# Dense work at the ends of attention heads, and decode scores in two PSUM banks

## The chip, the cores and the metric

The kernel runs on one core of a Trainium2 chip. The metric is the device time of one execution in microseconds (us); before the change it is 1550.55 us, the median of three runs (1549.25 to 1555.3).

## The reference

One inference step of a one-layer encoder with two kinds of input: a prompt of 1024 frames, and 8 decode streams with 16 new frames each and a cache of 512 past frames. The layer has two parallel head groups, 4 heads of differential softmax attention and 4 heads of retention; they come from one input projection and feed one output projection. A gated MLP with a convolution of width 3 follows, and a final RMSNorm. The part that the change touches is the attention:

```python
def diff_attention_block(q, k, v, q_pos, k_pos, rel_bias, lam):
    bias = ...                                                  # T5 buckets, per head
    visible = (k_pos[None, :] // CHUNK) <= (q_pos[:, None] // CHUNK)
    def probs(qi, ki):
        s = jnp.einsum('bqhd,bkhd->bhqk', qi, ki) * A_QK_DIM ** -0.5 + bias
        return jax.nn.softmax(jnp.where(visible, s, NEG_INF), axis=-1)
    p = probs(q[..., :64], k[..., :64]) - lam * probs(q[..., 64:], k[..., 64:])
    return jnp.einsum('bhqk,bkhd->bqhd', p, v)
# prompt: 8 query blocks of 128 for each head, over keys 0 .. end of the block
# decode: for each of 8 streams, 16 queries over 512 cached and 16 new keys
```

## The kernel before

TensorE (PE) takes its instructions in the order in which the code writes them from the start of the attention stage on (`manual_schedule` for PE). The order on the other engines and on the DMA queues is made by a planner that simulates the program; it can bring a load or a copy forward as far as buffers allow. SP issues most loads, ACT's queue the stores of evacuated rows.

Between the steps of attention and decode the code calls `fill(ns)`. It puts dense work, the input projections, on PE: units in a list, cut into steps of three matmuls. A step of a `k` or `q` unit (24 steps, 384 columns) is entered as 480 ns, one of a `kr`, `qr` or `gr` unit (72 steps, 256 columns) as 320 ns. `prog["lim"]` says how many units may have been started: where the limit is reached, `fill` puts nothing on PE. `drain(n)` does all steps until n units are done. `later(ns, fn)` writes `fn` when the entered time has moved on by ns. All dense work that attention and decode do not use is done in the retention stage that follows, where `fill` is called too, until it runs out.

Attention (lines 684 to 712) runs over 32 blocks, n_ = 8 * head + block. In each round it writes `scores` of the next block, a fill, `flip` of this block (transposes of the probabilities, L649), a fill, `weighted` (the product with V, L661), a fill. `scores` (L626) needs two PSUM buffers `sc`, one for each half of the differential softmax; DVE adds the bias (L629) and takes the maximum (L631), ACT the exponential (L632), DVE merges the halves (L637), and only then can `flip` run. After blocks 3 and 7 the four outputs are normalised and `heads_out` is due (`later`): 4 transposes (L670), a scaled copy on ACT (L672), and a store to d_m. Before the first block of the next head, `drain(2 * h2 + 2)` finishes that head's k and q units, and `load_v` loads its V into `vt`, of which there is one buffer. The two units that follow the k and q units, `kr` and `qr`, are done in the last head.

Then the pool of attention is closed and that of decode opened in its place. The last `qr` unit's weights are half in the new pool (`with_extra(dp)`); the cached keys of stream 0 (`kc`, 1 MB) go there too. `fill(9000)` covers their load. Decode runs over 8 streams. For each, `dflip` writes 4 transposes of the cached keys for each head (L744), copies them to SBUF (ACT for odd heads, L746, DVE for even, L748) and fills 400 after each head; then `dflip2` of the stream before (products of the probabilities `e` with `dm`, L773, and of its 16 new keys, L776), `dscore` (L756), a fill, `dout` of the stream before (L790), a fill. The PSUM buffers `tp` that L744, L773, L776 and L790 write are two.

In retention (line 988 on) the decode rows come first: for each of 8 streams a `fill(2000)`, 8 products with its state (L1018), 8 products for the new state (L1023), the update on DVE (L1026), the store, and the load of the state three streams on (L1044). There are three state buffers.

Of the kernel before, what the change touches and what calls it, by code (L numbers as in the profile page):

```python
# [7 lines left out]
F32 = mybir.dt.float32  # L8
# [3 lines left out]
ALU = mybir.AluOpType  # L12
# [36 lines left out]
def body(ctx: ExitStack, tc: tile.TileContext, i):  # L49
# [485 lines left out]
    with ExitStack() as st:  # L535
# [73 lines left out]
            units.append([lambda: load_wt(base, h * 128), lambda w_: dense_t(nm, h, w_), None])  # L609

        def load_v(h):
            vt = ap.tile([128, 8, 128], F32, tag="vt", bufs=1, name="vt")
            nc.sync.dma_start(vt, i["v_prompt"][:, h * 128:h * 128 + 128].rearrange("(t p) d -> p t d", p=128))
            return vt

# [39 lines left out]
        def weighted(h, vt, qb, e, sm, pTs):  # L655
            if qb % 4 == 0:
                o4s[0] = ap.tile([128, 4, 128], F32, tag="o4", bufs=2, name="o4")
            o4 = o4s[0]
            po = tp()[:, 0]
            for n in range(qb + 1):  # L660
                T.matmul(po[:, 0:128], lhsT=pTs[n // 4][:, n % 4], rhs=vt[:, n], start=(n == 0), stop=(n == qb))  # L661
            V.tensor_scalar_mul(o4[:, qb % 4], po[:, 0:128], sm[:, 4:5])
            if qb % 4 == 3:
                small_norm(ap, o4, 4)
                later(5000, lambda: heads_out(h, qb, o4))

        def heads_out(h, qb, o4):
            p_ = tp()
# [10 lines left out]
        def spare():  # L679
# [5 lines left out]
        drain(2)  # L685
        vt = load_v(0)
        cur = (0, vt, 0) + scores(0, kqs[0], 0)
        f_scores = ([1500, 1250, 1150, 1200, 650, 850, 450, 650],
                    [1950, 1850, 1750, 1650, 1550, 1450, 1350, 1250])
        f_flip = ([1925, 1775, 1625, 1475, 1325, 1325, 1475, 1025],  # L690
# [3 lines left out]
        for n_ in range(8 * NH):  # L694
            h, qb = divmod(n_, 8)
            nxt = None
            if n_ < 8 * NH - 1:
                h2, qb2 = divmod(n_ + 1, 8)
                if qb2 == 0:
                    drain(2 * h2 + 2)  # L700
                    vt = load_v(h2)
                nxt = (h2, vt, qb2) + scores(h2, kqs[h2], qb2)
            prog["lim"] = 10 if n_ >= 23 else n_ // 8 * 2 + 4
            fill(f_scores[h // 3][qb])
            pTs = flip(*cur)
            fill(f_flip[h // 3][qb])
            weighted(*cur, pTs)
            fill(f_out[h // 3][qb])
            cur = nxt
# [4 lines left out]
    with ExitStack() as st:  # L714
# [19 lines left out]
            nc.sync.dma_start(vn, i["v_sample"][b * TD:(b + 1) * TD])  # L734
            vcs[b] = vc, vn

        def dflip(b):
            KT = dp.tile([128, NH, PAST + TD], F32, tag="KT", bufs=2, name="KT")
            kc = kcs.pop(b)
            G.tensor_copy(KT[:, :, PAST:], knT[:, :, b * TD:(b + 1) * TD])  # L740
            for h in range(NH):
                p_ = tp()
                for n in range(4):
                    T.transpose(p_[:, n], kc[:, n, h * 128:h * 128 + 128], ident)  # L744
                if h % 2:
                    S.copy(KT[:, h, 0:PAST], p_.rearrange("p a b -> p (a b)"))  # L746
                else:
                    V.tensor_copy(KT[:, h, 0:PAST], p_.rearrange("p a b -> p (a b)"))  # L748
                fill(400)
            return KT  # L750

        def dscore(b, KT):
            s_ = pva.tile([128, 1024], F32, tag="sc", bufs=2, name="sc")
            for (c0, c1) in ((0, 512), (512, 528)):
                for h in range(NH):
                    T.matmul(s_[32 * h:32 * h + 32, c0:c1], lhsT=qbd[:, h, b].rearrange("p a t -> p (a t)"),  # L756
                             rhs=KT[:, h, c0:c1], start=True, stop=True, skip_group_check=True)
            sm = dp.tile([128, 4], F32, tag="sm", bufs=3, name="sm")
            nk = PAST + TD
            V.tensor_tensor(out=s_[:, 384:nk], in0=s_[:, 384:nk], in1=nbs, op=ALU.add)  # L760
            V.tensor_reduce(out=sm[:, 0:1], in_=s_[:, 0:nk], op=ALU.max, axis=AX.X, negate=True)
            e = dp.tile([128, nk], F32, tag="e", bufs=2, name="e")
            S.activation(out=e, in_=s_[:, 0:nk], func=ACTF.Exp, bias=sm[:, 0:1], scale=1.0, accum_out=sm[:, 1:2])
            V.reciprocal(out=sm[:, 2:3], in_=sm[:, 1:2])
            dm = dp.tile([128, 128], F32, tag="dm", bufs=1, name="dm")
            V.tensor_scalar(out=dm, in0=seld, scalar1=sm[:, 2:3], scalar2=lamcol, op0=ALU.mult, op1=ALU.mult)
            return e, dm
# [40 lines left out]
        load_k(0)  # L808
        prog["rope"] = dp.tile([128, NT, 2, 64], F32, name="rope")
        nc.sync.dma_start(prog["rope"], i["rope"].rearrange("(t p) a d -> p t a d", p=128))  # L810
        fill(9000)
        nbs = dp.tile([128, 144], F32, name="nbs")
        p_ = tp().rearrange("p a b -> p (a b)")
        T.matmul(p_[:, 0:144], lhsT=anti16[0:64], rhs=hk, start=True, stop=True)
# [2 lines left out]
        for b in range(NB + 1):  # L817
            if b < NB:
                if b + 1 < NB:
                    load_k(b + 1)  # L820
                load_vc(b)
                KT = dflip(b)
            if last:
                pT = dflip2(*last)
            fill(0)
            nxt = (b,) + dscore(b, KT) if b < NB else None
            fill(1200 if b else 1500)
            if last:
                dout(last[0], pT)
            fill(1000)  # L830
            last = nxt
        while pend:
            fill(500)
# [818 lines left out]
```

## Time and profile before

| | |
|---|---|
| median of three runs | 1550.55 us |
| the profiled execution | 1549.34 us |
| its span | 1547.6 us |
| PE busy | 1509.1 us, 98% of the span |
| DVE, ACT, POOL busy | 963.7 us, 600.7 us, 232.3 us |
| chain that ended last, by engine | PE 86%, DVE 5%, DMA 4% |

The span is the time from the first to the last instruction in the profile. PE is busy nearly everywhere, so the change can only move the time by the idle time of PE that it closes or opens, and by what PE itself has more or less to do. Attention reaches from about 184 to 457 us, decode from there to about 557 us, retention to about 650 us.

### The profile page before, as it was taken

What the parts mean: (1) busy time and instruction counts of PE and PEld (TensorE: products, weight loads), DVE (VectorE), ACT (ScalarE), POOL (GpSimd) and SP (SyncE); (2) the same over time, 40 slices, a digit from 0 to 9 for tenths busy, and PEclk for the clock granted to TensorE, in tenths of its full rate; (3) what the DMA queues carried; (4) which work ended last, traced back from release to release, by engine and by line L of the source; (5) the groups of instructions that cost most, each with busy time, mean ns of one, the idle gap of its engine ahead of it and who ended that gap; (6) DMA issues with size and microseconds to landing.
All of it is one profiled execution on the core that took longest, in us unless ns stands there. A gap on an engine that the chain in (4) does not pass through costs nothing.

```text
span 1547.6 us, 27019 instructions
## 1 busy us (share of the span) xinstructions
PE 1509.1 (98%) x10580; PEld 1375.5 (89%) x10580; DVE 963.7 (62%) x1735; ACT 600.7 (39%) x1167; POOL 232.3 (15%) x335
## 2 busy tenths in 40 slices
PE   6999999999999999999999999999999999999998
PEld 5867899999998999888899999999999988888786
DVE  5701247888864533653489777877787758254695
ACT  4501125555322432555565443444444345021212
POOL 2000021111221111433202101110111100000051
PEclk9999999999999999999999999999999999999999
DMA  9965331111329655685532222222222238132232
GB/s 296 276 253 182 114 104 49 55 51 53 107 83 328 226 201 176 221 259 194 176 117 87 70 79 77 75 71 79 72 79 71 79 112 276 36 116 87 95 134 109
DMA packets 191515, 205.98 MB, mean 133 GB/s; under 512 B 11357, under 2 KB 149899, under 8 KB 191388
## 3 DMA queue, kind: packets, MB, share of 16 engines
q1 hardware_dynamic: 172412, 189.31, 37.5%
q10 hardware_dynamic: 18976, 14.95, 3.0%
q8 instruction: 83, 1.36, 0.3%
q14 instruction: 44, 0.36, 0.1%
HBM read 154.66 MB, written 49.56 MB: 132 GB/s over the span
## 4 chain that ended last, share of the span: by engine, by line
PE 86%; DVE 5%; DMA 4%; ACT 1%; SPq 1%; issue 1%; POOL 0%; ACTq 0%; POOLq 0%; DVEq 0%
PE dn L62 10%; PE dn L64 10%; PE dn L63 10%; PE pb L1339 5%; PE pb L1341 5%; PE pb L1340 5%; PE pf L64 3%; PE pf L62 3%; PE pf L63 3%; PE dn L1339 2%; PE dn L1341 2%; PE dn L1340 2%; PE tp L1339 2%; PE tp L1341 2%; PE tp L1340 2%; PE tp L63 2%
## 5 line engine op out<-in xcount | busy, mean ns | idle before, releaser
L62 PE MATMUL dn<-w,hhi 128*128 128x256 f32 x648 | 190.1, 293 | 0.0
L64 PE MATMUL dn<-w,hlo 128*128 128x256 f32 x648 | 181.6, 280 | 0.0
L63 PE MATMUL dn<-w,hhi 128*128 128x256 f32 x648 | 181.4, 280 | 0.0
L62 PEld LDWEIGHTS dn<-w,hhi 128*128 128x128 f32 x648 | 122.4, 189 | 12.0 <-issue 10.2
L64 PEld LDWEIGHTS dn<-w,hlo 128*128 128x128 f32 x648 | 122.4, 189 | 7.5 <-issue 7.5
L63 PEld LDWEIGHTS dn<-w,hhi 128*128 128x128 f32 x648 | 122.5, 189 | 4.3 <-issue 4.2
L1285 DVE SCALAR_TENSOR_TENSOR y<-U,cv,y 128x1168 f32<-128x1168 f32 x88 | 124.3, 1429 | 3.0 <-ACT y L1282 2.1
L58 ACT CAST sl<-raw 128x512 fp32r<-128x512 f32 x65 | 40.3, 622 | 108.2 <-PE pb L1340 93.5
L58 ACT CAST se<-raw 128x512 fp32r<-128x512 f32 x66 | 41.0, 624 | 100.5 <-PE dn L1340 48.4
L62 PE MATMUL dn<-hhi,w 128*128 128x384 f32 x192 | 69.4, 361 | 0.0
L246 POOL TENSOR_TENSOR sg<-sg,rot 128x256 f32<-128x256 f32 x36 | 28.1, 781 | 272.1 <-DVE rot L245 230.4
L64 PE MATMUL dn<-hhi,w 128*128 128x384 f32 x192 | 64.6, 336 | 0.0
L63 PE MATMUL dn<-hlo,w 128*128 128x384 f32 x192 | 64.5, 336 | 0.0
L1291 POOL COPY tails<-U 128x18 f32<-128x18 f32 x44 | 23.1, 526 | 270.8 <-DVE U L1356 182.1
L1282 ACT ACTIVATE y<-U,cv 128x1168 f32<-128x1168 f32 x44 | 60.2, 1367 | 4.5 <-DVE U L1360 0.5
L1511 DVE TENSOR_TENSOR facc<-facc,pf 128x512 f32<-128x512 f32 x54 | 36.8, 681 | 39.1 <-PE pf L64 39.0
L59 DVE TENSOR_TENSOR w<-raw,w 128x512 fp32r<-128x512 f32 x56 | 38.9, 709 | 35.7 <-ACT w L58 23.6
L632 ACT ACTIVATE e<-sc,sm 128x128 f32<-128x128 f32 (+7 forms) x64 | 47.4, 744 | 30.9 <-DVE sm L631 30.1
L62 PE MATMUL dn<-woh,mh 128*128 128x512 f32 x144 | 57.9, 402 | 0.0
L58 ACT CAST ew<-wr 128x512 fp32r<-128x512 f32 x24 | 14.6, 618 | 109.5 <-PE tp L63 85.5
L58 ACT CAST w<-raw 128x512 fp32r<-128x512 f32 x56 | 33.3, 619 | 60.5 <-PE dn L63 33.8
L64 PE MATMUL dn<-woh,ml 128*128 128x512 f32 x144 | 56.5, 393 | 0.0
(424 smaller groups left out, 4871.2 us busy)
## 6 DMA issues: line engine op xcount, KB each, us to landing
wa<-in_w_ada SPq DMA_DIRECT2D x48, 512.0 KB, 8.5
raw<-in_w_up SPq DMA_DIRECT2D x88, 256.0 KB, 3.0
raw<-in_w_in SPq DMA_DIRECT2D x56, 256.0 KB, 4.1
wr<-in_w_down SPq DMA_DIRECT2D x48, 256.0 KB, 3.3
gr<-d_g SPq DMA_DIRECT2D x20, 576.0 KB, 3.5
d_g<-y SPq DMA_DIRECT2D x22, 512.0 KB, 2.6
kc<-in_cache_k SPq DMA_DIRECT2D x8, 1024.0 KB, 7.1
vc<-in_cache_v SPq DMA_DIRECT2D x8, 1024.0 KB
```

The costliest lines, as they stand in the source:

```text
L58: S.copy(hi, src)
L59: V.tensor_tensor(out=lo, in0=src, in1=hi.bitcast(F32), op=ALU.subtract)
L62: T.matmul(out, lhsT=sh, rhs=mh, start=first, stop=False)
L63: T.matmul(out, lhsT=sh, rhs=ml, start=False, stop=False)
L64: T.matmul(out, lhsT=sl, rhs=mh, start=False, stop=last)
L632: S.activation(out=e[:, hf, 0:nk], in_=s_[:, 0:nk], func=ACTF.Exp, bias=sm[:, hf:hf + 1], scale=1.0, accum_out=sm[:, 2 + hf:3 + hf])
L1282: S.activation(out=y[:, j0:j1], in_=U[:, j0:j1], func=ACTF.Identity, scale=wconv[0][:, kt:kt + 1], bias=bconv[:, kt:kt + 1])
L1285: V.scalar_tensor_tensor(out=y[:, j0:j1], in0=U[:, j0 + j:j1 + j], scalar=wconv[j][:, kt:kt + 1], in1=y[:, j0:j1], op0=ALU.mult, op1=ALU.add)
L1339: T.matmul(o, lhsT=sh, rhs=mh, start=st_, stop=False, skip_group_check=True)
L1340: T.matmul(o, lhsT=sh, rhs=ml, start=False, stop=False, skip_group_check=True)
L1341: T.matmul(o, lhsT=sl_, rhs=mh, start=False, stop=en, skip_group_check=True)
L1511: V.tensor_tensor(out=facc[t][:, sl], in0=facc[t][:, sl], in1=p_, op=ALU.add)
```

## The change

- `vt` has two buffers instead of one.
- `heads_out` is due 8000 ns after `weighted`, not 5000.
- After the first `scores` the limit is set to 4 units and `fill(2400)` is called.
- The limit rises in the last block of a head (`(n_ + 1) // 8`), not in the first block of the next.
- Decode: `fill(11500)` instead of `fill(9000)` ahead of the first stream; `dflip2` of the stream before moves between the transposes of head 1 and those of head 2; a fill of 700 stands ahead of `dscore`; `dout` follows `dscore` with nothing between; the fill behind is 1500 (2500 for stream 0) instead of 1000.
- `dscore` writes its 528 columns as two halves of 264, each in a PSUM bank of its own, instead of 512 and 16. The bias, the maximum and the exponential go over a view of two times 264.

```diff
-            vt = ap.tile([128, 8, 128], F32, tag="vt", bufs=1, name="vt")
+            vt = ap.tile([128, 8, 128], F32, tag="vt", bufs=2, name="vt")
...
-                later(5000, lambda: heads_out(h, qb, o4))
+                later(8000, lambda: heads_out(h, qb, o4))
...
         cur = (0, vt, 0) + scores(0, kqs[0], 0)
+        prog["lim"] = 4
+        fill(2400)
...
-            prog["lim"] = 10 if n_ >= 23 else n_ // 8 * 2 + 4
+            prog["lim"] = 10 if n_ >= 23 else (n_ + 1) // 8 * 2 + 4
...
+        NK2 = (PAST + TD) // 2
+
-        def dflip(b):
+        def dflip(b, mid):
...
+                if h == 1:
+                    mid()
                 fill(400)
...
-            s_ = pva.tile([128, 1024], F32, tag="sc", bufs=2, name="sc")
-            for (c0, c1) in ((0, 512), (512, 528)):
+            sb_ = pva.tile([128, 1024], F32, tag="sc", bufs=2, name="sc").rearrange("p (z c) -> p z c", z=2)
+            for z in range(2):
                 for h in range(NH):
-                    T.matmul(s_[32 * h:32 * h + 32, c0:c1], lhsT=qbd[:, h, b].rearrange("p a t -> p (a t)"),
-                             rhs=KT[:, h, c0:c1], start=True, stop=True, skip_group_check=True)
+                    T.matmul(sb_[32 * h:32 * h + 32, z, 0:NK2], lhsT=qbd[:, h, b].rearrange("p a t -> p (a t)"),
+                             rhs=KT[:, h, z * NK2:(z + 1) * NK2], start=True, stop=True, skip_group_check=True)
...
-            V.tensor_tensor(out=s_[:, 384:nk], in0=s_[:, 384:nk], in1=nbs, op=ALU.add)
-            V.tensor_reduce(out=sm[:, 0:1], in_=s_[:, 0:nk], op=ALU.max, axis=AX.X, negate=True)
+            s_ = sb_[:, :, 0:NK2]
+            V.tensor_tensor(out=sb_[:, 1, 384 - NK2:NK2], in0=sb_[:, 1, 384 - NK2:NK2], in1=nbs, op=ALU.add)
+            V.tensor_reduce(out=sm[:, 0:1], in_=s_, op=ALU.max, axis=AX.XY, negate=True)
...
-            S.activation(out=e, in_=s_[:, 0:nk], func=ACTF.Exp, bias=sm[:, 0:1], scale=1.0, accum_out=sm[:, 1:2])
+            S.activation(out=e.rearrange("p (z c) -> p z c", z=2), in_=s_, func=ACTF.Exp, bias=sm[:, 0:1], scale=1.0,
+                         accum_out=sm[:, 1:2])
...
-        fill(9000)
+        fill(11500)
...
-                KT = dflip(b)
+            pTs = []
+
+            def mid():
+                if last:
+                    pTs.append(dflip2(*last))
+
+            if b < NB:
+                KT = dflip(b, mid)
+            else:
+                mid()
+            fill(700 if b < NB else 1300)
+            nxt = (b,) + dscore(b, KT) if b < NB else None
             if last:
-                pT = dflip2(*last)
-            fill(0)
-            nxt = (b,) + dscore(b, KT) if b < NB else None
-            fill(1200 if b else 1500)
-            if last:
-                dout(last[0], pT)
-            fill(1000)
+                dout(last[0], pTs[0])
+            fill(1500 if b else 2500)
             last = nxt
```

## Rows read from the trace of the kernel before

**Rows 1.** The page: busy us (share of the span) and instructions of each engine.
```profile
PE 1509.1 (98%) x10580; PEld 1375.5 (89%) x10580; DVE 963.7 (62%) x1735; ACT 600.7 (39%) x1167; POOL 232.3 (15%) x335
```

**Rows 2.** Waits of PE from 235 to 470 us: total us, times, longest.
```profile
PE tp L670 <- DVE sm L635: 2.2, 1, 2.2
...
PE tp L661 <- ACT pT L651: 1.1, 3, 0.4
PE tp L661 <- DMA vt<-out_v_prompt: 0.7, 1, 0.7
```

**Rows 3.** Timeline of PE behind the first scores: start, us, instruction [idle before].
```profile
239.96 0.39 PE L626 MATMUL sc<-khi,qs 128*128 128x256 f32 x1 [1.67 <-ACT e L632]
...
240.65 0.34 PE L62 MATMUL dn<-hhi,w 128*128 128x384 f32 x1
...
241.18 0.33 PE L62 MATMUL dn<-hhi,w 128*128 128x384 f32 x1
```

**Rows 4.** Timeline, end of head 0: scores of block 7, its merge on DVE, its flip.
```profile
276.50 0.48 PE L626 MATMUL sc<-khi,qs 128*128 128x512 f32 x1
...
284.04 1.27 DVE L637 SCALAR_TENSOR_TENSOR e<-e,sm 128x1024 f32<-128x1024 f32 x1
...
285.46 1.06 PE L649 MATMUL tp<-ident_all,e 128*128 128x128 f32 x8
```

**Rows 5.** Timeline, end of head 2: the same three of block 23.
```profile
374.81 0.48 PE L626 MATMUL sc<-khi,qs 128*128 128x512 f32 x1
...
383.51 1.28 DVE L637 SCALAR_TENSOR_TENSOR e<-e,sm 128x1024 f32<-128x1024 f32 x1
...
384.94 0.74 PE L649 MATMUL tp<-ident_all,e 128*128 128x128 f32 x5
```

**Rows 6.** Timeline from the last heads_out to the first transposes of decode.
```profile
455.47 0.60 PE L670 MATMUL tp<-ident_all,o 128*128 128x128 f32 x4
...
458.95 1.14 ACT L58 CAST w<-raw 128x512 fp32r<-128x512 f32 x2 [2.15 <-DMA d_m<-om]
...
460.26 2.43 DVE L59 TENSOR_TENSOR w<-raw,w 128x512 fp32r<-128x512 f32 x3
...
468.99 1.11 PE L744 MATMUL tp<-ident_all,kc 128*128 128x128 f32 x4 [2.50 <-DMA kc<-in_cache_k]
```

**Rows 7.** Windows: length, busy PE, PEld, DVE, ACT, POOL, PE clock, DMA, GB/s.
```profile
465.00:470.00 5.00, 2.50 (x16) 2.15 (x16) 0.31 (x1) 0.00 (x0) 0.00 (x0) 0.85 1.07 359
470.00:475.00 5.00, 5.00 (x44) 4.30 (x43) 3.67 (x10) 2.68 (x5) 0.73 (x1) 0.81 1.05 372
```

**Rows 8.** Timeline of PE in one decode stream, from dflip2 to dout.
```profile
500.92 1.05 PE L773 MATMUL tp<-dm,e 128*128 128x128 f32 x8
501.90 0.28 PE L776 MATMUL tp<-dm,e 128*16 128x128 f32 x1
...
503.13 0.39 PE L62 MATMUL dn<-w,hhi 128*128 128x256 f32 x1
...
503.94 0.28 PE L62 MATMUL dn<-w,hhi 128*128 128x256 f32 x1
...
504.28 0.28 PE L62 MATMUL dn<-w,hhi 128*128 128x256 f32 x1
...
504.71 1.08 PE L790 MATMUL tp<-vc,pT 128*32 128x128 f32 x32
```

**Rows 9.** Timelines of DVE and ACT in the same stream: `dm`, and a copy of L746.
```profile
505.74 0.84 DVE L766 TENSOR_SCALAR dm<-ident_all,sm,lamcol 128x128 f32<-128x128 f32 x1
...
500.77 0.59 ACT L746 COPY KT<-tp 128x512 f32<-128x512 f32 x1 [1.29 <-PE tp L744]
```

**Rows 10.** Retention: products of stream 4, the load for stream 7, and loads' landing (median).
```profile
595.57 1.06 PE L1018 MATMUL rt<-sb,Qd 128*32 128x128 f32 x8
...
601.36 0.37 SPq L1044 DMA_DIRECT2D sb<-in_state_ret  x1
...
sb<-in_state_ret SPq DMA_DIRECT2D x5, 256.0 KB, 2.9
```

## The prediction

> **What bounds the kernel now.** I read the page first. PE is busy for 98% of the span [rows 1], so outside a few holes the kernel lasts as long as PE has work, and no part of that work is taken away: dense steps that are written earlier are missing later. What the change can move is therefore idle PE. The second view was PE's own waits from the start of attention to the first stream of decode; third the timelines around each of them, with DVE's beside PE's, because a hole that is filled with dense work uncovers the chain on DVE that the dense work had hidden; fourth the clock by window. The reader is to see five holes: 1.67 us behind the first scores [rows 3], 0.4 and 0.7 us at the ends of heads 0 to 2, 2.2 us at a `heads_out` [rows 2], and 2.50 us in front of decode [rows 6]. After the last the granted clock is 0.85 and 0.81 in two windows of 5 us [rows 7]. In decode itself PE has no wait.
>
> **The change part by part.** A `k` or `q` step costs 241.18 - 240.65 = 0.53 us of PE [rows 3], a `kr`, `qr` or `gr` step 504.28 - 503.94 = 0.34 us [rows 8]. The counts of steps below come from the numbers in the code.
>
> *Start.* The second `scores` waits until the exponential frees its PSUM buffer. `fill(2400)` puts 5 steps there, 2.6 us, more than the 1.67 us. Their weights are those of the third unit, which the three pairs of weight buffers let the planner load early. I take -1.7 us; the bounds are 0 (weights late) and -1.9.
>
> *Ends of heads.* With 5 steps spent at the start, and later 5 in each last block, each head runs out of dense work three steps into block 6: what stood between the scores and the flip of block 7 is thinned. For head 0 it was 480 + 1920 + 1440 entered ns, 8 steps; it becomes 480 + 960 + 480 + 480, 5 steps, and `heads_out` of block 3 (4 transposes, about 0.4 us) comes in because of its 8000. Flip 7 begins 0.15 us after DVE's merge ends (284.04 + 1.27 = 285.31, flip at 285.46 [rows 4]): DVE's chain of 8.8 us from the first score is already as long as PE's 8.96. PE now arrives 1.2 us sooner and waits that out, unless DVE is faster; DVE is nearly full there, so I take the whole wait. In return two steps stand between flip and `weighted`, over the copies that PE waited for (0.4), and the second `vt` buffer removes the 0.7 [rows 2]. Head 0: +0.1. Head 1 has the copies' wait but no `vt` wait: +0.8. Head 2 is worse, since block 23 could already take dense work before: 5 steps fewer than the 8, 2.6 us, less `heads_out`, against a chain that ends at 383.51 + 1.28 = 384.79 for a flip at 384.94 [rows 5]; if DVE does its weight splits later, part is regained: +1.3 of at most +2.2. In blocks 13 and 21 one step less may uncover 0.3 more. Sum: +2.5 us, between -1 (DVE's chain shortens by as much as PE comes early) and +3.5.
>
> *`heads_out` later.* The wait of 2.2 us [rows 2] comes from normalised rows that are not ready; 3000 more entered ns are 9 steps of 0.34, 3.1 us. It goes: -2.2 us, bound 0 if other steps get late by it. ACT, SP and d_m behind it are read only in decode's pool and much later.
>
> *Before decode.* `fill(11500)` adds 8 steps, 2.7 us, over the wait of 2.50 us for the keys. With it goes the slow clock, stretches at 1.2 instead of 2.4 GHz: in the second window (1 - 0.81) x 5 = 0.95 us of PE's work is lost, and in the first, where PE works only from 468.99, up to half of that last us, 0.5 [rows 6, 7]; 1.4 us together. Elsewhere waits of 1.67 and 2.2 us left the clock at full. But `heads_out` of the last block now comes 9 steps later in the dense stream, and the pool of decode opens only when its store has landed: the cast of the last `qr` unit's weights waited for d_m until 458.95, their lower halves came from 460.26 on [rows 6]. Before, 17 steps of the older unit lay between `heads_out` at 455.47 and the first step that needs these weights (455.8 + 17 x 0.34 = 461.6); now 8 do (458.6). The weights are there no sooner than 460.3: a new hole of about 1.7 us. The keys are issued from the same moment as before, so what the new hole takes is time that they use too, and they are covered. Sum: -2.5 - 1.4 + 1.7 = -2.2 us; bounds -3.9 (weights were not gated) and 0.
>
> *Decode.* Scores: 16 matmul instructions before (each product in fp32 is two), 16 after, over 528 columns either way; what goes is 8 instructions with 16 columns, up to a quarter of the 501.90 to 503.13 [rows 8], at most 0.3 us a stream; what comes is that the two L776, which ran beside the scores, stand alone, up to 0.2. A change between dense and other work costs 0.09 us (0.43 from 504.28 to L790 for three matmuls of 0.34 [rows 8]); `dout` directly behind `dscore` and `dflip2` directly behind head 1 make five blocks of such work a stream where there were six. That is -0.2 us a stream. The view of two times 264 costs DVE and ACT the same elements, here hidden by dense work. Against it stand two new chances to wait. L776's buffer is freed by ACT's copy of head 1, 0.59 us and its start [rows 9], and L773 covers only 0.98 (501.90 - 500.92 [rows 8]): up to 0.2. And `dm` must be ready sooner: after the scores' end at 503.13 it took until 506.58 at most (505.74 + 0.84 [rows 9]), 3.5 us, with `dout`, 1500 and two heads, about 4.3 us of PE, over it; before, it had 8. I take -0.1 a stream for 7 streams, -0.7 us; bounds -3 and +7.
>
> The Trainium skill (TensorEngine Tiling (Array Packing), Key Properties) says that a change of tiling mode, not of tile, drains TensorE. The 0.09 us agrees with it. By that rule only changes between full width and 32 columns count, and L776 is 32 columns wide: four changes a stream before, four after, so the neighbours bring nothing and decode would come to about 0 instead of -0.7.
>
> *Retention.* More entered work is used up earlier (45,700 instead of 41,900 in decode, 3000 more at the end of attention, less 500), so the last 20 dense steps before are missing here: streams 5, 6 and 7 of the decode rows have none. PE's own work for one is 2.1 us (two times 1.06 [rows 10]). The state of stream 7 is loaded after that of stream 4 is stored: issue at 601.36, 2.9 us to land, 8.7 us after stream 4 began at 595.57 [rows 10]. PE would be there 6.2 us after: a wait of about 2 us in all. Taken +2.0, bounds 0 (earlier loads) and +3.
>
> **Sum.** -1.7 + 2.5 - 2.2 - 2.2 - 0.7 + 2.0 = -2.3 us against the profiled execution of 1549.3 us (span 1547.6 and 1.7 around it): 1547.0. That execution is 1.2 us under the median of the runs, so the median comes to 1548.2 us.
>
> **The rivals.**
>
> *All holes close* (faster). DVE's chains shorten because evacuations and weight splits leave them, and decode's weights are not gated: start 1.7, `vt` and copies 1.1, `heads_out` 2.2, keys and clock 3.9, decode 2.5, together -11.4: 1539 us. For it: two of the evacuations of a `q` unit lie in the chain of block 7 now and would move out. Against: DVE's load is the same, and the last block's evacuation comes in.
>
> *The holes only move* (no change). Each wait filled is paid back at flips, at the pool's opening and in retention: 1550.5 us, within 1 us. For it: 0.15 us of slack at both flips [rows 4, 5]. Against: the 2.2 us wait and the slow clock have no counterpart later.
>
> *The middle `dflip2` stalls* (slower). Its two PSUM buffers are those of the heads' transposes, and `dm` has lost half its time. If DVE or ACT is late by a rotation of `qr` rows or a weight split, PE stands in every stream, and each stall delays the next scores. At 1.1 us for 7 streams it costs 7.7 us, beside the sum without decode's gain (-1.6): 1556.6 us. It turns the sign from 0.25 us a stream on. Against: in the stream shown both were in time.
>
> **How the numbers follow.** Forecast (1544 to 1551) 0.45, all close 0.25, only move 0.16, middle stalls 0.14. The range 1538 to 1556 takes in the first, most of the second, the third and half of the fourth. About 0.5% (7.8 us) is what a measurement of this kernel can tell from no change. Faster by more: nearly all of the second case, 0.25. Slower by more: a third of the fourth and a rest, 0.08. The same: 0.67.
>
> **What would show it.** In the profile after: no wait at the second scores, at L670 or for `vt`; waits of L649 on L637 at three head ends, 1 us or more; a wait of dense PE work on the splits of weights just before decode, none for the keys, and no window with a clock under 1.00 there; in decode no wait at L773 or L776 over 0.3 us; in retention a wait of L1018 for a state's load. The forecast is wrong if the flips don't wait, if the dense work before decode runs through, or if PE waits in each stream.

## The result and the profile after

The changed kernel takes 1592.26 us (median of four runs, 1589.97 to 1594.32); the kernel before took 1549.9 us beside it. The ratio is 1.0248, 95% interval 1.0228 to 1.0268: slower by about 40 us, where 1548.2 us and a range of 1538 to 1556 were forecast. PE has as many instructions as before; its busy time grows by 18 us and its idle time by 27 us. Line 1 of the page after, beside [rows 1] (columns as there):

```profile
PE 1527.3 (96%) x10580; PEld 1386.6 (87%) x10580; DVE 966.2 (61%) x1735; ACT 604.7 (38%) x1171; POOL 233.0 (15%) x335
```

Most of the added busy time is work at the lower clock (15 of the 18 us, by the fourth column below). So each stretch of both traces is split in four: its length, the time in which PE waited (gaps of over 0.1 us between its instructions), the work lost to the clock (half of the time at 1.2 GHz in which PE worked), and the dense steps of 320 ns that fall into it. Times in us, before / after; the decode rows end where the products behind them begin, the rest ends with PE's last instruction. The trace of `m_busy`, an execution of 2138 us at a clock of 0.65, is left out here and in all that follows.

| stretch | length | waits | lost to clock | dense steps | more, with 0.34 a step taken out |
|---|---|---|---|---|---|
| start, to the first scores | 237.7 / 240.0 | 9.3 / 11.7 | 2.8 / 4.7 | same | +2.3 |
| attention, to the last flip | 208.4 / 221.7 | 6.2 / 14.3 | 0 / 3.4 | same | +13.3 |
| entry, to decode's first transposes | 22.9 / 36.4 | 2.5 / 6.3 | 0 / 3.0 | 48 / 65 | +7.7 |
| decode, to the last `dout` | 82.3 / 88.9 | 0 / 4.5 | 1.5 / 0 | 99 / 102 | +5.5 |
| end of decode, to the first product of retention | 14.4 / 21.2 | 0 / 3.3 | 0 / 3.3 | 40 / 40 | +6.9 |
| decode rows of retention | 46.7 / 48.8 | 0 / 4.8 | 0 / 5.2 | 66 / 46 | +8.9 |
| the rest | 928.1 / 928.3 | 5.3 / 5.3 | 1.7 / 1.8 | same | +0.3 |

The start is the same program on PE in both kernels; in the traces of the runs below it takes 237.6 to 241.5 us, so its 2.3 us are within the scatter of single executions. The other five stretches each lose something, and each has its own row.

*Attention.* Waits of PE after, from 236 to 463 us (total us, times, longest), to be held against [rows 2]: the waits for `vt` and at L670 are gone as forecast, but the flips wait for DVE's merge seven times. At the ends of heads the scores of the next head (L626) also wait, for the exponential that frees their buffer.

```profile
PE tp L649 <- DVE e L637: 8.3, 7, 2.2
PE sc L626 <- ACT e L632: 2.6, 4, 1.6
PE tp L661 <- ACT pT L651: 1.8, 3, 1.0
PE tp L558 <- ACT kf L596: 1.6, 2, 0.8
```

The end of head 0 after, which answers to [rows 4] (timelines of PE, DVE and ACT):

```profile
280.78 0.39 PE L626 MATMUL sc<-khi,qs 128*128 128x512 f32 x1
...
288.43 0.30 PE L626 MATMUL sc<-khi,qs 128*128 128x128 f32 x1 [1.61 <-ACT e L632]
...
291.74 1.09 PE L649 MATMUL tp<-ident_all,e 128*128 128x128 f32 x8 [1.36 <-DVE e L637]
```

```profile
283.44 2.34 DVE L631 TENSOR_REDUCE sm<-sc 128x1 f32<-128x1024 f32 x2
...
286.95 0.68 DVE L59 TENSOR_TENSOR w<-raw,w 128x512 fp32r<-128x512 f32 x1
...
288.46 0.42 DVE L585 SCALAR_TENSOR_TENSOR qs<-dn,qs 64x256 fp32r<-64x256 f32 x1
...
290.40 1.28 DVE L637 SCALAR_TENSOR_TENSOR e<-e,sm 128x1024 f32<-128x1024 f32 x1
```

```profile
285.79 1.12 ACT L58 CAST w<-raw 128x512 fp32r<-128x512 f32 x2
...
287.09 1.10 ACT L632 ACTIVATE e<-sc,sm 128x1024 f32<-128x1024 f32 x1
```

Before, the merge ended 8.8 us after the first score; now it ends 10.9 us after (290.40 + 1.28 - 280.78). DVE did not get slower: splits of the next unit's weights (L59), the evacuation of the `q` unit (L585) and the next head's maxima now stand in its queue ahead of the merge, where the splits came behind it before. A smaller part comes by way of ACT: a cast of weights (L58) now stands between the two exponentials, and the second ends 7.4 us after the first score, where it ended 6.8 us after it before.

*Entry.* Three timelines of after, PE, DVE and SP, in answer to [rows 6]:

```profile
474.24 0.60 PE L670 MATMUL tp<-ident_all,o 128*128 128x128 f32 x4
...
478.40 0.35 PE L62 MATMUL dn<-w,hhi 128*128 128x256 f32 x1 [0.48 <-ACT w L58]
...
479.42 0.38 PE L63 MATMUL dn<-w,hhi 128*128 128x256 f32 x1 [0.67 <-DVE w L59]
...
480.56 0.39 PE L63 MATMUL dn<-w,hhi 128*128 128x256 f32 x1 [0.17 <-DVE w L59]
...
490.53 0.55 PE L62 MATMUL dn<-w,hhi 128*128 128x256 f32 x1 [4.97 <-DVE rot L245]
```

```profile
489.56 0.42 DVE L242 TENSOR_TENSOR sg<-dn,rope 128x256 f32<-128x256 f32 x1 [9.06 <-DMA rope<-in_rope]
```

```profile
479.31 0.45 SPq L730 DMA_DIRECT2D kc<-in_cache_k  x1
479.81 0.50 SPq L818 DMA_DIRECT2D rope<-in_rope  x1
```

The three small waits are those forecast for the weights, 1.3 us. The fourth was not: the evacuation of this unit needs the rope table, which lands 9.8 us after its issue behind the keys. Two tiles fill both `dn` buffers, and the third cannot start. The trace of before had the warning: there the first such evacuation waited too, with the keys' wait beside it. That row of DVE before:

```profile
471.25 0.43 DVE L242 TENSOR_TENSOR sg<-dn,rope 128x256 f32<-128x256 f32 x1 [0.42 <-DMA rope<-in_rope]
```

*Decode.* Waits of PE after, from 500 to 592 us (before: none):

```profile
PE tp L781 <- DVE KT L752: 2.7, 3, 1.7
PE tp L781 <- DVE dm L774: 0.8, 1, 0.8
PE tp L781 <- DVE rstd L131: 0.7, 1, 0.7
PE tp L784 <- ACT KT L750: 0.3, 1, 0.3
```

*End of decode and retention.* PE, ACT and SP after; the rows of L1032 answer to L1018 of [rows 10]. The last unit's weights lie half in retention's pool, so their cast waits for decode's end; `d_m` is stored at 592.53. (The row names the store of `d_gr` that was issued 0.5 us later; in `j_fill8500` below the same cast is put down to `d_m`.) Before, a long rest of the older unit covered that. The state of stream 7 is issued at 644.25 behind three loads of `w_out`, and is there at 649.5, 5.3 us later and not 2.9:

```profile
595.72 0.58 PE L62 MATMUL dn<-w,hhi 128*128 128x256 f32 x1 [3.14 <-ACT w L58]
...
642.80 1.43 PE L1032 MATMUL rt<-sb,Qd 128*32 128x128 f32 x8 [1.53 <-DMA sb<-in_state_ret]
...
649.51 1.92 PE L1032 MATMUL rt<-sb,Qd 128*32 128x128 f32 x8 [3.28 <-DMA sb<-in_state_ret]
```

```profile
595.05 1.14 ACT L58 CAST w<-raw 128x512 fp32r<-128x512 f32 x2 [2.05 <-DMA d_gr<-sg]
```

```profile
592.53 0.38 SPq L849 DMA_DIRECT2D d_m<-om  x1
...
642.64 1.51 SPq L1093 DMA_DIRECT2D raw<-in_w_out  x3
644.25 0.41 SPq L1058 DMA_DIRECT2D sb<-in_state_ret  x1
```

Behind most of these waits the clock falls. Windows of after (columns as in [rows 7]): clock 0.77 and 0.89 behind the flip of block 13, 0.50 and 0.84 behind the rope table, 0.56 behind the weights, 0.50 twice behind the states.

```profile
330.00:335.00 5.00, 2.99 (x14) 2.70 (x13) 3.96 (x7) 3.32 (x7) 0.00 (x0) 0.77 0.00 0
335.00:340.00 5.00, 5.00 (x29) 4.70 (x29) 2.41 (x6) 0.50 (x2) 0.00 (x0) 0.89 0.00 0
...
490.00:495.00 5.00, 4.47 (x21) 4.50 (x22) 3.54 (x8) 1.86 (x3) 1.87 (x2) 0.50 1.05 380
495.00:500.00 5.00, 5.00 (x36) 4.72 (x36) 1.81 (x5) 0.41 (x1) 0.73 (x1) 0.84 1.06 383
...
595.00:600.00 5.00, 4.14 (x17) 3.84 (x18) 1.89 (x3) 1.66 (x3) 0.00 (x0) 0.56 0.76 234
...
645.00:650.00 5.00, 1.72 (x9) 1.36 (x9) 0.88 (x4) 0.00 (x0) 1.04 (x1) 0.50 0.80 252
650.00:655.00 5.00, 5.00 (x22) 4.25 (x21) 1.65 (x6) 1.14 (x8) 1.01 (x1) 0.50 0.10 20
```

### The profile page after: what moved, and what is told of

Same layout as the page of the kernel before. It is cut to its first block, busy times and chain, and to the rows that moved or that the text cites. A ratio compares the mean times of both kernels' runs of the same rounds, so it can differ in the third digit from the quotient of the medians.

```text
span 1592.4 us, 27037 instructions
## 1 busy us (share of the span) xinstructions
PE 1527.3 (96%) x10580; PEld 1386.6 (87%) x10580; DVE 966.2 (61%) x1735; ACT 604.7 (38%) x1171; POOL 233.0 (15%) x335
## 4 chain that ended last, share of the span: by engine, by line
PE 84%; DVE 6%; DMA 4%; ACT 3%; issue 2%; SPq 1%; POOL 0%; ACTq 0%; POOLq 0%; DVEq 0%
PE dn L62 10%; PE dn L64 10%; PE dn L63 9%; PE pb L1353 5%; PE pb L1354 5%; PE pb L1355 5%; PE pf L64 3%; PE pf L62 3%; PE pf L63 3%; PE dn L1353 2%; PE dn L1355 2%; PE dn L1354 2%; PE tp L1353 2%; PE tp L1355 2%; PE tp L1354 2%; PE tp L63 2%
## 5 line engine op out<-in xcount | busy, mean ns | idle before, releaser
L62 PE MATMUL dn<-w,hhi 128*128 128x256 f32 x648 | 192.0, 296 | 8.6 <-DVE rot L245 5.0
L63 PE MATMUL dn<-w,hhi 128*128 128x256 f32 x648 | 184.0, 284 | 1.0 <-DVE w L59 0.8
L62 PEld LDWEIGHTS dn<-w,hhi 128*128 128x128 f32 x648 | 124.8, 193 | 22.7 <-issue 17.9
L63 PEld LDWEIGHTS dn<-w,hhi 128*128 128x128 f32 x648 | 124.9, 193 | 6.0 <-issue 4.2
L58 ACT CAST sl<-raw 128x512 fp32r<-128x512 f32 x65 | 40.4, 623 | 107.1 <-PE pb L1354 98.4
L58 ACT CAST se<-raw 128x512 fp32r<-128x512 f32 x66 | 41.0, 623 | 100.2 <-PE dn L1354 48.1
L58 ACT CAST w<-raw 128x512 fp32r<-128x512 f32 x56 | 33.2, 618 | 77.6 <-DMA raw<-in_w_in 38.5
L59 DVE TENSOR_TENSOR w<-raw,w 128x512 fp32r<-128x512 f32 x56 | 38.5, 707 | 37.6 <-ACT w L58 25.5
L63 PE MATMUL dn<-wol,mh 128*128 128x512 f32 x144 | 56.1, 390 | 0.0
```

What stands on the lines that cost most here:

```text
L58: S.copy(hi, src)
L59: V.tensor_tensor(out=lo, in0=src, in1=hi.bitcast(F32), op=ALU.subtract)
L62: T.matmul(out, lhsT=sh, rhs=mh, start=first, stop=False)
L63: T.matmul(out, lhsT=sh, rhs=ml, start=False, stop=False)
```

## The experiments

Ratios are to the kernel before, measured on the same chip at the same time (1551.7 to 1552.8 us), with their 95% intervals. In the diffs "after" is the changed kernel; names are those of the change.

### Each half by itself, and two repairs

Before, with the attention half alone (`vt` in two buffers, 8000, the limit and `fill(2400)`):

> The kernel before with the attention half of the change alone (two vt buffers, heads_out 8000 entered ns late, five dense steps at the start and in each last block); decode as before. Theory M (many holes, each with the slow clock that follows it; the dense work is spent too early): the flips at the ends of heads wait as in the changed kernel, attention 11 us longer; the entry to decode also waits, for the weights' lower halves (1.3 us) and for the rope table (about 5 us), some 5 us more than before; the gr unit left for the end of decode is 2500 entered ns shorter but still covers it (0); retention loses dense work in streams 6 and 7 (2 us). Together +18 us: 1563 to 1573 us. Rival D (the loss is decode's new order and its two banks): the attention half costs what its waits cost and no more, +2 to +6 us: 1552 to 1556 us, and the changed kernel's other 36 us come with the decode half.

Before, with the decode half alone (two banks, order, fills):

> The kernel before with the decode half alone (two banks of 264, the weighted values directly behind the scores, the middle call of dflip2, the new fills, fill(11500) in front). Theory M: entry +2 to +3 us, since 17 steps of the old unit and 16 of the qr unit end at about 467 and the rope table lands at 471 (a wait of about 4 us with a slow clock behind it, where the keys' 2.5 us and its clock were); decode +3 to +4 us of waits at the middle dflip2; the end of decode has 3600 entered ns of gr left in place of 7400 (0 to +1); retention lacks 12 dense steps (+3 to +5). Together about +10 us: 1557 to 1564 us. Rival D: nearly the whole loss, 1582 to 1590 us. Should the order of decode be a gain as predicted, decode's own stretch is shorter than the 82.3 us of before.

After, with heads_out as early as before:

```diff
-                later(8000, lambda: heads_out(h, qb, o4))
+                later(5000, lambda: heads_out(h, qb, o4))
```

> The changed kernel with heads_out 5000 entered ns late again, as before. Theory M: the last heads_out waits for its rows again (+2.2 us), but nine steps more of the old unit lie over the opening of decode's pool: the waits for the weights go (-1.3), the wait for the rope table falls from 5.0 to about 3.3, and nine steps of gr more are left for the end of decode, where the hole of 3.1 us and the slow clock behind it shrink (-3 to -5), and for retention (-2 to -6). Together -5 to -14 us: 1578 to 1587 us. Rival D: 1590 to 1595 us (the 2.2 us come back and nothing else changes).

After, with the rope table issued ahead of the keys:

```diff
-        load_k(0)
         prog["rope"] = dp.tile([128, NT, 2, 64], F32, name="rope")
         nc.sync.dma_start(prog["rope"], ...)
+        load_k(0)
```

> The changed kernel with the load of the rope table issued ahead of the first load of keys. Theory M: the two dense accumulators in front of decode are full because their rotation waits for the table; with the table in 3 to 5 us sooner PE's wait of 4.97 us there goes and with it the slow clock behind it (3 us of PE's work); the keys still land in time. 1583 to 1587 us. Rival K (the hole only moves to the keys, which land later): PE waits 3 to 5 us at the transposes of the keys instead, the clock falls there, 1590 to 1594 us.

Measured: attention half 1570.37 us, 1.0109 (1.0079 to 1.0139); decode half 1565.46 us, 1.0083 (1.0057 to 1.0108). Theory M had 1563 to 1573 and 1557 to 1564 (a little low), rival D is out: neither half carries the loss. The halves make 1.9% together, both at once 2.5%: there is a share that only both together cost. Heads_out at 5000 gives 13 us back: 1579.2 us, 1.0163 (1.0134 to 1.0192), within M's range. In its trace the wait at the end of decode is 0.3 us and the clock there stays at full; the wait for the rope table is 4.3 us and not M's 3.3.

The rope table was a miss: 1590.59 us, 1.0233 (1.0199 to 1.0267), no measurable gain. M's mechanism is there in the trace: the entry is 6.8 us shorter (29.6 against 36.4), with no low clock, and PE has no wait for the keys, where rival K had 3 to 5 us. Of the wait for the table 0.9 us is left. The transposes of the second head wait 0.7 us for DVE's copy of `nbs`, which stands behind three splits of weights:

```profile
489.30 2.42 DVE L59 TENSOR_TENSOR w<-raw,w 128x512 fp32r<-128x512 f32 x3
491.64 0.29 DVE L823 COPY nbs<-tp 128x144 f32<-128x144 f32 x1
```

But decode is 2.0 us longer, with 6.4 us of waits where it had 4.5 (1.5 us of them again for a rotation of a `qr` tile), the decode rows of retention are 0.8 us longer and the stretches behind them, where the programs are the same, 2 us. Part of what one hole gave back went into the next; the rest is not told from scatter.

### The parts of the attention half, and the banks alone

Each is the kernel before with one edit.

```diff
         cur = (0, vt, 0) + scores(0, kqs[0], 0)
+        prog["lim"] = 4
+        fill(2400)
```

> The kernel before with the five dense steps at the start alone. In the attention half alone attention was 11.8 us longer, with eight flips waiting for DVE's merge. Theory L (the raised limit of the last blocks thins the dense work of the blocks before it at every head): the start takes 1.7 us of wait away and gives up to 2.6 back at the end of head 0, nothing afterwards; attention 207 to 210 us against 208.4, total 1549 to 1553 us. Theory S (the five steps shift every later block of the planner, so that DVE's order is worse at all heads): attention 215 us or more, total 1557 us or more.

```diff
-            prog["lim"] = 10 if n_ >= 23 else n_ // 8 * 2 + 4
+            prog["lim"] = 10 if n_ >= 23 else (n_ + 1) // 8 * 2 + 4
```

> The kernel before with the raised limit of the last blocks alone (the next head's dense steps start one block earlier). Theory L: five steps fewer in the sixth and following blocks of heads 1 and 2, and the rotation of dense evacuations falls into DVE's chains: waits of flips at 13, 15, 21, 23 as in the attention half; attention 214 to 219 us, total 1556 to 1562 us. Theory S: attention 206 to 210 us, total 1548 to 1553 us.

Two `vt` buffers and 8000 for 5000:

> The kernel before with two vt buffers and heads_out 8000 entered ns late. If the later heads_out is what opens the holes in front of decode (theory M): attention loses its waits for vt and at L670, 3 us shorter or less; the entry to decode waits 1.3 us for the weights and 4 to 5 us for the rope table, with a slow clock of some 1.8 us of work behind it, where 2.5 us of keys and 1.5 us of clock were; retention lacks nine dense steps, 1 to 3 us. Total 1553 to 1558 us. As predicted blind (the wait at L670 goes, nothing is late by it): 1547 to 1550 us.

`dscore` of the changed kernel in the decode of before:

> The kernel before with the scores of decode in two banks of 264 columns alone, in the old order with the old fills. By the trace of the changed kernel a stream's scores take 0.91 us of PE where they took 1.22: 8 x 0.3 = 2.4 us less in decode, total 1547.5 to 1549.5 us. Should the view of two times 264 cost DVE and ACT, or the middle products their place beside the scores (1.4 us over the streams), the total is 1550 to 1553 us.

Measured: start 1556.99 us, 1.0030 (1.0018 to 1.0043); limit 1564.57 us, 1.0069 (1.0045 to 1.0094); `vt` and heads_out 1557.52 us, 1.0034 (1.0022 to 1.0047); banks 1552.93 us, 0.9997 (0.9983 to 1.0012). The limit cost more than theory L gave it. The start alone makes attention 215.9 us long, as theory S had it, yet not by S's way: the new waits are all at the end of head 0, and heads 1 to 3 have those of before. Waits of its PE from 236 to 300 us:

```profile
PE tp L649 <- DVE sm L634: 2.8, 1, 2.8
PE sc L626 <- ACT e L632: 1.6, 1, 1.6
PE tp L661 <- ACT pT L651: 1.0, 1, 1.0
PE tp L649 <- DVE e L637: 0.9, 1, 0.9
```

That is 6.3 us of waits; the kernel before has 3.0 in the same stretch, the 1.67 at the second scores [rows 3] among them. Behind the last of them the clock falls, for some 3 us of work. The limit does the same to heads 1 and 2 (its flips 13, 15, 21, 23 wait 2.3, 1.2, 2.3 and 1.2 us).

With heads_out late and everything else as before, the entry has the new holes: 1.3 us for weights and 3.35 us for the rope table, where the keys' 2.5 us were. M's 1553 to 1558 us holds, the blind 1547 to 1550 does not.

The banks alone are nothing that can be measured, and their trace says why: a stream's scores, with the two products of the new keys beside them as before, take 1.21 us (504.15 to 505.36), against 1.23 in [rows 8] (501.90 to 503.13). The 0.91 us of the changed kernel (533.20 to 534.11), from which this run's expectation was worked out, are scores without these two products, which take 0.32 us a stream by themselves there.

```profile
504.15 0.28 PE L780 MATMUL tp<-dm,e 128*16 128x128 f32 x1
...
505.36 0.39 PE L62 MATMUL dn<-w,hhi 128*128 128x256 f32 x1
```

### The rope table, the work left behind, retention, the order in decode

Before, without the table and with two `vt` buffers:

```diff
-        prog["rope"] = dp.tile([128, NT, 2, 64], F32, name="rope")
-        nc.sync.dma_start(prog["rope"], ...)
```

> The kernel before without the rope table in decode's pool (each rotation loads its own 64 KB, as the first qr unit does) and with two vt buffers. Theory Q (the 576 KB of the table share the queues with the first keys, and that is why the keys land at 469): the keys land 2 to 3 us sooner, PE's wait of 2.50 us in front of decode falls under 0.7 and with it the slow clock behind it, the waits for vt go (0.7): 1546 to 1549 us. Rival (the keys' time is their own, or the small loads hold up the later keys and values in the queue): the wait stays over 2 us or waits for kc and vc come up in decode, 1551 to 1556 us.

After, with nine dense steps fewer in front of decode:

```diff
-        fill(11500)
+        fill(8500)
```

> The changed kernel with fill(8500) for fill(11500) in front of decode, so that nine dense steps more are left behind decode; heads_out stays 8000 late. Theory G (the ten microseconds by which both halves together cost more than one and the other come from too little dense work left: the last gr unit's weights are gated by the end of decode's pool, and the streams of retention are uncovered): the wait of 3.1 us at the end of decode falls under 0.5 and the slow clock behind it goes (3.3 us of work), retention's waits for the state fall from 4.8 to about 2.4 and its slow clock is halved; the wait for the rope table in front of decode stays, about 5 us. 1578 to 1584 us. Rival H (the late heads_out costs by its own place): no change at the end of decode, 1589 to 1594 us.

Before, with 20 steps of retention done ahead of its first flip:

```diff
         load_t(0)
-        fill(9000)
+        fill(15400)
```

> The kernel before with 20 dense steps of retention moved ahead of its first flip (fill(15400) for fill(9000)), so that the streams 5 to 7 of the decode rows have none; nothing else is changed. As predicted blind, this costs the two waits for the state's load, 2 us: 1552 to 1555 us. Theory M (waits for the state of 4.8 us as in the changed kernel, and the clock falls behind them for some 5 us of work): 1557 to 1563 us.

The decode half, with the middle products behind head 3:

```diff
-                if h == 1:
+                if h == 3:
                     mid()
```

> The decode half alone with the weighting products of the stream before put back behind the fourth head's transposes (mid at h == 3); the scores still stand directly before the weighted values, the fills are those of the changed kernel. Theory W (the products stand too early for dm, and for the buffer that ACT or DVE frees): decode's waits at the products, 3.0 us in the decode half, go to under 0.5; the wait for the rope table in front of decode stays. 1560 to 1564 us. Rival (the waits come from evacuations on DVE and ACT that fall into each stream, wherever the products stand): waits of 2 to 3 us remain, 1564 to 1568 us.

Measured: without the table 1553.77 us, 1.0000 (0.9988 to 1.0011). The keys' wait is 2.48 us as before, and theory Q's gain is not there. But the run does not part Q from its rival: the DMA engines are as full as before (share 1.05 and 1.06 from 465 to 475 us, 1.07 and 1.05 in [rows 7]), since the next stream's keys are issued at 464.22 in the table's place, where it was 467.59.

Nine steps more left behind decode: 1579.51 us, 1.0169 (1.0147 to 1.0190), 13 us less than after, within theory G's range, with heads_out as late as in after. So what only both halves together cost is mostly the shortage behind decode: at the end of decode the traces of the halves wait 0.2 and 0.3 us, that of after 3.3. Its waits from 470 to 660 us, first lines: the 3.1 us at the end of decode are gone, the states' 4.8 us are 2.4, and the rope table's 5.0 are 2.3, which G had left at 5: some 4 of the 13 us come from the entry.

```profile
PE rt L1032 <- DMA sb<-in_state_ret: 2.4, 1, 2.4
PE dn L62 <- DVE rot L245: 2.3, 1, 2.3
PE tp L784 <- ACT KT L750: 1.3, 2, 1.0
```

Bare streams in retention (without dense work between them), alone: 1559.63 us, 1.0047 (1.0029 to 1.0066), +7 us where the blind prediction said +2. The waits are 1.38 and 5.32 us, and the clock falls behind them (windows, below).

Middle products at their old place: 1565.97 us, 1.0091 (1.0069 to 1.0113), no better than the decode half, and its decode waits 3.8 us. Theory W falls: in the places where PE waits, DVE or ACT is late with copies, wherever the products stand.

### The order at equal work, the clock, and a better version

Bare streams again, with 12 and 44 products that nothing reads ahead of streams 6 and 7:

```diff
                     fill(2000)
+                    if b > 5:
+                        pz = dn()
+                        for _ in range(12 if b == 6 else 44):
+                            T.matmul(pz[:, 0:256], lhsT=hs(hhi, 0, 0), rhs=hhi[:, 1, 0:256], start=True, stop=True)
```

> The kernel of k_ret (20 dense steps of retention moved ahead, the last streams bare) with products added that nothing reads: 12 of 256 columns ahead of stream 6 and 44 ahead of stream 7, 1.4 and 5.0 us of PE, about as long as the two waits for the state's loads there (1.38 and 5.32 us). The loads come no sooner, so the waiting time is merely filled. Theory C (the clock falls because PE idles): the granted clock stays at 1.00 through retention, the 3.9 us of work that k_ret loses there are back, 1554 to 1557 us. Rival N (the clock falls for another reason, or the waits alone are the whole price): 1558 to 1563 us, slow stretches as in k_ret.

The same kernel again, for its trace:

> The kernel of m_busy again, for a trace of the undisturbed program: products that nothing reads fill PE's waits for the state's loads in streams 6 and 7. Theory C (the clock falls because PE idles): granted clock 1.00 in all of retention, waits there under 0.7 us in all, retention's streams as long as in k_ret less its 3.9 us lost to the clock, about 45.5 us in place of 49.4; total 1554 to 1557 us. Rival N: slow stretches in retention as in k_ret, 1558 to 1563 us.

Bare streams (first fence) and the same with products in the waits (second), windows as in [rows 7]:

```profile
602.00:607.00 5.00, 3.62 (x29) 2.91 (x28) 1.76 (x8) 0.00 (x0) 0.00 (x0) 1.00 1.01 303
607.00:612.00 5.00, 1.06 (x8) 0.78 (x7) 0.88 (x4) 0.00 (x0) 1.04 (x1) 0.58 0.94 273
612.00:617.00 5.00, 3.62 (x16) 3.02 (x16) 0.17 (x1) 1.14 (x8) 0.24 (x1) 0.50 0.09 28
617.00:622.00 5.00, 5.00 (x27) 4.78 (x27) 2.86 (x7) 1.17 (x2) 0.76 (x1) 0.56 0.60 192
```

```profile
602.00:607.00 5.00, 5.00 (x40) 4.23 (x38) 0.88 (x4) 0.38 (x1) 0.00 (x0) 1.00 0.49 133
607.00:612.00 5.00, 5.00 (x40) 4.35 (x40) 1.76 (x8) 0.00 (x0) 0.00 (x0) 1.00 1.02 314
612.00:617.00 5.00, 5.00 (x43) 4.88 (x43) 0.88 (x4) 0.00 (x0) 1.04 (x1) 1.00 0.91 262
617.00:622.00 5.00, 5.00 (x42) 4.49 (x41) 1.47 (x6) 1.16 (x9) 0.56 (x1) 1.00 0.15 36
```

The first fence has the low clock from the second window on; in the second the clock stays at full where PE is kept at work, and the stretch of the decode rows takes 46.3 us in place of 49.4. So in this stretch the low clock is a consequence of the waits: the waits of 6.7 us cost 3 us more than their length. The totals alone do not show it: 1558.99 us, 1.0029 (1.0014 to 1.0043), and 1559.14 us, 1.0038 (1.0025 to 1.0051), against 1.0047 (1.0029 to 1.0066); the expected 1554 to 1557 was not reached, and the 4 us by which the start differs from run to run cover the gain.

The decode half with the dense work of before:

```diff
-        fill(11500)
+        fill(9000)
...
-            fill(700 if b < NB else 1300)
+            fill(700)
...
-            fill(1500 if b else 2500)
+            fill(1500 if b else 1800)
```

> The decode half alone with the dense work cut to what the kernel before enters: fill(9000) in front, 700 behind the last streams and 1800 behind the first, so that the new order and the two banks stand alone. Theory E (the half's 13 us are mostly the work spent too early): entry as before (the keys' wait of 2.5 us), retention as before; of decode's part the own work of +1.9 us stays and some of the 3.0 us of waits: 1553 to 1557 us. Rival D (order and banks are the cost): 1561 to 1567 us. As predicted blind (order and banks gain 0.7 us): 1550 to 1552 us.

Measured 1556.51 us, 1.0022 (1.0012 to 1.0033), as theory E had it: order and banks cost 3 us by themselves, and the other 0.6% of the decode half is dense work spent too early. Its decode waits 2.5 us, mostly for `dm` and for keys.

Before, with two `vt` buffers, `fill(10600)` in front of decode and `fill(1750)` for each stream of retention:

> The kernel before with two vt buffers, five dense steps more over the keys' wait in front of decode (fill(10600), just short of the third qr tile, which would need the rope table) and the steps of retention spread as 1750 a stream in place of 2000, so that the last stream keeps some. If holes are the price: the keys' wait falls to about 0.8 us and the slow clock behind it goes (1.4 us), vt's 0.7 goes, retention has no wait: 1547 to 1550 us. If the five steps are missed elsewhere: 1551 to 1555 us.

Measured 1551.93 us, 1.0004 (0.9994 to 1.0013): the keys' wait and the low clock behind it are gone, and 1.7 us of wait for a rotation and 0.8 us of small ones come in decode. No version tried here beats the kernel before.

## Why the prediction was wrong

- **Start, -1.7.** Right by itself: the wait went.
- **Ends of heads, +2.5 (at most +3.5).** This step failed first. The sum assumed that DVE's chain stays 8.8 us long while PE comes sooner. It grew to 10.9 us at block 7, and from 8.6 and 7.8 to 10.6 and 10.4 at blocks 13 and 21, where the sum had 0.3 us and the flips wait 2.0 and 2.2. At block 7 the planner put splits, evacuations and the next head's maxima ahead of the merge, at blocks 13 and 21 an evacuation and the next block's maximum. (At block 23, where the sum had 1.3, the chain did not grow and the flip waits 0.7.) The text named the opposite case (DVE's chain shortens) as a bound and not this one. Nor had the sum the wait of the next head's scores for the exponential, 1.6 us behind block 7. Attention's waits rose by 8.1 us and the clock took 3.4 more; the last 1.8 us are longer products and transposes on lines that wait now (L626, L649, L558). The five steps at the start, costed with this at -1.6 (-1.7, and +0.1 at head 0), cost 0.30% alone.
- **heads_out later, -2.2.** The wait at L670 went, as it should. The sum left out what the nine steps had been: the cover of the pool's opening, and then work for later stages. Alone, with `vt`, it cost 0.34%.
- **Before decode, -2.2.** The hole for the gated weights was there, 1.3 us for 1.7; the keys' wait went. The rope table was missed, although its row stood in the trace (0.42 us of DVE, hidden by the keys' wait): 5.0 us, and 3.0 us to the clock. "What is late next" was asked of the weights and keys, not of the tiles that the added steps would finish.
- **Decode, -0.7.** The eight instructions with 16 columns, priced at up to 0.3 us a stream, cost nothing that shows: with the banks alone a stream keeps 1.21 of its 1.23 us. In the changed kernel the scores take 0.91 us, but the two products of the new keys, which ran beside them, stand alone now and take 0.32: 1.23 again. Over the streams the order adds 1.9 us at the transposes of the keys (L744 took 11.4 us of PE with the clock taken out, L748 takes 13.3) and 0.6 at L781. With that, and waits that the range (-3 to +7) allowed and the third rival described, order and banks come to +3 us. By the rule of the Trainium skill (TensorEngine Tiling (Array Packing), Key Properties) the term would have been about 0; what is measured is above both, by waits and by the longer transposes, of which that rule says nothing. The 0.09 us that the prediction read as agreeing with it is no sign of it: between full-width transposes a step of three matmuls takes 0.43 us too (499.70 to 500.13 in the trace of before).
- **End of decode, no term.** The same kind of gate as at decode's pool, costed there and not looked for here: +6.9 us.
- **Retention, +2.0 (at most +3).** The 20 bare steps were right to the step, and so was the wait for the state. Its size was not: the load queued behind those of `w_out` and took 5.3 us, and the waits of 4.8 us were followed by 5.2 us of work lost to the clock.
- **The clock.** The prediction took from two waits of 1.67 and 2.2 us that such waits leave the clock alone, and had it only as a gain. In the changed kernel it falls behind waits of 2.0 and 2.2 us too. And the reading was that of one execution: the 1.67 us at the second scores stand in 11 of the traces, and behind them the clock falls in five (`b_dec`, `f_lim`, `l_mid3`, `n_order`, `o_best`) and stays in six.

Of the rivals, the third (the middle products wait) was there at 0.6 us a stream and not 1.1; "the holes only move" had the mechanism of most steps, but not that a moved hole grows. All four cases shared the premise that filled waits are worth about their length, so none reached over 1556.6.

What is shown by experiment: the share of the start, the limit and the late heads_out, the order at equal work, the shortage behind decode, the bare streams, and the clock behind the waits in retention. That the longer DVE chains come from the planner's order is read from the traces; no run forced the old order on DVE. How much of attention's loss is the clock was not separated either: it was 0, 1.7, 3.4 and 3.4 us in four traces with the same 14 us of waits (`j_fill8500`, `a_attn`, after, `d_ropefirst`).

## What to carry to other kernels

Dense work that fills gaps is a stock: each step moved to an earlier gap has to be followed to the place where it is missing, and there one asks which buffer, pool or load it had been covering. When a wait on the bound engine is closed, list for every operand that the added steps read or write when it lands or comes free, also those whose wait is hidden now by a longer one. Where the order of another engine is made by a planner, its chain length is no constant of the sum.

## What the runs showed of the hardware

In 17 traces there are 37 waits of PE of 2 us and more between 236 and 665 us. Behind 28 of them the granted clock fell within 5 us, and 3 more lay in a stretch that was slow already; a wait of 3.35 us with two `vt` buffers and a late heads_out left it at 1.00. So the low clock is usual after such a wait and not certain. Dense work in the place of the waits kept it at 1.00 in retention (`p_busy`). Before decode the 16 DMA engines are full (share 1.05 to 1.11), and there the keys landed no sooner when the table's load was taken away and the next keys came in its place (a wait of 2.48 us against 2.50).
